# Two layers of a hybrid block on one core: residual chains split by urgency, with wide residuals and weights split ahead

## The chip, the cores and the metric

The kernel runs on one core of one Trainium2 chip. The metric is the device time of one execution in microseconds; runs are compared by their median. A core has TensorE (PE, the matmuls), VectorE (DVE), ScalarE (ACT), GpSimd (POOL), and SyncE (SP), which issues most DMAs. TensorE's clock has two levels, 1.2 and 2.4 GHz; the profile shows the granted clock as a share of the higher.

## What is computed

The input is 16 meta tokens and 512 tokens of width 1024, in float32. Two layers follow, each of the same form (cut from the reference; `s5_mixer`, `swa_attention` and `mla_mixer` are a complex linear recurrence over the tokens, attention in a window of 128, and attention with compressed keys and values):

```
for l in range(DEPTH):                                   # 2
    a = rms_norm(h, norm_pre_mix[l])
    u, q, k, v, cq, ckv, kr = split(a @ w_in[l])
    mixed = concat(rms_norm(s5_mixer(u), g_s5), rms_norm(swa_attention(q, k, v), g_swa),
                   rms_norm(mla_mixer(cq, ckv, kr), g_mla))
    h = h + rms_norm(mixed @ w_out[l], norm_post_mix[l])
    a = rms_norm(h, norm_pre_mlp[l])
    f = square(relu(a @ w_mlp_up[l])) @ w_mlp_down[l]    # 1024 -> 4096 -> 1024
    h = h + rms_norm(f, norm_post_mlp[l])
return h[:, 16:]
```

A norm multiplies by the reciprocal root of the mean square over the 1024 features of each token, and by a gain for each feature.

## The kernel before

**Layout.** All activations lie with features on the 128 partitions: `h` is 128 x 8 x tokens (feature 128k + p). The tokens go in two halves, A with 272 and B with 256, so each product has 272 or 256 columns. A norm's sum over the features is a matmul against a column of ones (`colsum`, L205) after the eight squared slices were added up: Squares on ScalarE, additions on VectorE (L200).

**Products.** A weight block is 128 outputs by 1024 inputs; each of its halves is one DMA of 128x512 floats (`raw`, issued by SP, L130). A float32 product is made of three fp32r products: ScalarE copies the half to the rounded `hi`, VectorE subtracts it to get `lo` (the split, L135, named `w`), and TensorE runs hi x hi, hi x lo, lo x hi, so 12 matmuls per half and 24 per block (L163, named `d` or `bu`). Activations are split in the same way: `gains` gives hi on ScalarE, with the gain as its scale, and lo on VectorE (L173, eight of each), `split` does it for the MLP's inner values (L170, `slot<-rl`). Some products of the first layer run in plain float32 (L155).

**Chains.** Between the products stand chains that use VectorE and ScalarE alone, but for the column sum:
- `norm_in(l, half)`: gains, sum of squares, column sum, reciprocal root `r`; `w_in` needs the gains first, and `r` when its columns are evicted (L403, L421, L447).
- `chain_mid(l, half)` after w_out: sum of squares over w_out's results (`big`), column sum, root (L215 to L217), `residual`, gains, then sum of squares and column sum of the new `h`.
- `chain_end(l, half)` after the MLP: the same up to `residual`, with a square more (L879, L881).

`residual` takes, for each of eight slices, one multiplication by `r` (L791) and one multiplication by the gain with addition to `h` (L792):

```
V.tensor_tensor(src[:, k, :n], src[:, k, :n], r[:, :n], op=ALU.mult)
V.scalar_tensor_tensor(h[hf][:, k, o:o + n], src[:, k, :n], sm(l, gn, k), h[hf][:, k, o:o + n], ...)
```

**Order.** The program is written as generators. `weave(main, sides)` takes steps of a main stream of products and, for every microsecond of its estimated cost, lets the side streams spend `rate` microseconds: the S5 recurrence (`RS`), the attentions (`RA`), the preparation of the next layer's S5 tables (`RP`). A scheduler at build time then orders each engine's instructions by the place where they were written and by priority: a part in `tc.high_priority(offset=HP)` is moved ahead by that offset; all chains have HP = 100, weight splits HW = 50. Each engine works through its list in order.

One layer runs so: norm and w_in of half A (11 blocks); w_in of half B; w_out of A; chain_mid of A; up and part of down of A's first MLP chunk; w_out of B; chain_mid of B; the chunks of the MLP (four of 8 up and 8 down blocks), first for B alone, then A and B together, then A alone. The last B blocks of a layer (`late`) run in the next layer: CU = 6 of them between the next layer's norm_in of A and its w_in, the rest behind that w_in. Half B's chain_end and norm_in of layer 1 run under w_out(1,0). In layer 1, w_in of B stands behind w_out(1,0) and chain_mid(1,0) (`WB[1] = 0`), and its first two blocks are the S5 input u, evicted by L421; S5 then takes transposes (L499, `y`), its input product (L513, `bu`), the recurrence on VectorE (L518 to L544, the scan at L534) and its output product (L557).

**Buffers named below.** `raw`, `w`: a weight half and its split. `slot`: split activations. `rl`: two buffers of 128x272 in the MLP. `ch`: three rows of a chain. `big0`, `big1`: results of w_out and of the MLP, by half. `kv`: the attention's keys and values of a layer.

The functions, with the profile's line numbers:

## Time and profile before

| | us |
|---|---|
| median of 3 runs | 1291.93 (1291.27 to 1293.69) |
| the profiled execution | 1289.2 |
| its span | 1287.4 |
| TensorE busy | 1217.5 (95%) |
| VectorE busy | 868.7 (67%) |
| ScalarE busy | 848.6 (66%) |
| chain that ended last, by engine | PE 47%, DVE 6%, ACT 2% |

A time in square brackets at the end of a timeline's row is how long the engine had stood before it, and the arrow names what ended that. Rows with "x8" hold eight instructions in a row; their time goes from the start of the first to the end of the last, and successive instructions overlap a little on one engine. TensorE's busy time counts matmuls at the lower clock in full.

### The profile page before, as it was taken

To read this page: it belongs to the slowest core of one execution; us is meant where nothing else is said; L and a number is where in the kernel's file an instruction comes from. 1 tells how busy PE (TensorE), PEld (TensorE's weight loads), DVE (VectorE), ACT (ScalarE), POOL (GpSimd) and SP (SyncE) were. 2 spreads that over 40 slices of the span, in tenths; PEclk is the share of its full clock that TensorE was granted. 3 is DMA by queue.
4 is the path that set the end of the run, shared out by engine and by line. 5 is a ranking of instruction groups with operands and counts; after the bars stand their busy time and mean duration, and the time that the engine had idled before them with its cause. 6 is when DMAs were issued, how large, how long until landed. Compare 5 with 4: busy or idle time off the path is not lost.

```text
span 1287.4 us, 27466 instructions
## 1 busy us (share of the span) xinstructions
PE 1217.5 (95%) x10256; PEld 1133.8 (88%) x10256; DVE 868.7 (67%) x2056; ACT 848.6 (66%) x1977; POOL 41.9 (3%) x103
## 2 busy tenths in 40 slices
PE   6999998999999999799999986999999999999995
PEld 4787876899999999788999985778989999999985
DVE  7888768789656656857766787766685333344775
ACT  6787777987764666766786674798675532534662
POOL 4000002000000000000000000000000000000000
PEclk9999998999999999899999996999999999999998
DMA  7223423254666656433456641314646332334652
GB/s 225 83 83 100 149 67 91 82 179 131 193 181 173 179 168 179 116 122 92 125 162 185 194 147 33 108 58 123 181 148 189 91 97 86 97 100 129 186 184 85
DMA packets 93237, 170.55 MB, mean 132 GB/s; under 512 B 10960, under 2 KB 14032, under 8 KB 93104
## 3 DMA queue, kind: packets, MB, share of 16 engines
q1 hardware_dynamic: 90288, 161.62, 42.3%
q0 software_dynamic: 2816, 7.18, 1.7%
q8 instruction: 81, 1.33, 0.4%
q14 instruction: 52, 0.43, 0.1%
HBM read 166.66 MB, written 2.10 MB: 131 GB/s over the span
## 4 chain that ended last, share of the span: by engine, by line
PE 47%; DVE 6%; ACT 2%; issue 1%; DMA 1%; DVEq 0%; ACTq 0%
PE d L163 33%; PE bu L163 7%; PE o L763 1%; DVE h L792 1%; DVE big L791 1%; PE pt L739 1%; PE s L680 1%; PE s L715 1%; DVE w L135 1%; PE bu L513 1%; DMA raw<-in_wblk 1%; ACT ch L126 1%; DVE slot L173 1%; PE o L205 1%; ACT w L126 0%
## 5 line engine op out<-in xcount | busy, mean ns | idle before, releaser
L163 PE MATMUL d<-slot,w 128*128 128x256 f32 (+1 forms) x6984 | 914.4, 289 | 22.1 <-ACT rl L126 6.2
L163 PEld LDWEIGHTS d<-slot,w 128*128 128x128 f32 x6984 | 867.5, 190 | 47.9 <-issue 11.9
L135 DVE TENSOR_TENSOR w<-raw,w 128x512 fp32r<-128x512 f32 x582 | 400.1, 690 | 214.7 <-ACT w L126 206.8
L126 ACT ACTIVATE w<-raw 128x512 fp32r<-128x512 f32 x582 | 364.1, 627 | 254.8 <-PE d L163 174.6
L170 DVE TENSOR_TENSOR slot<-rl,slot 128x256 fp32r<-128x256 f32 (+1 forms) x128 | 54.0, 427 | 62.4 <-ACT slot L126 60.6
L163 PE MATMUL bu<-slot,w 128*128 128x256 f32 x768 | 92.9, 280 | 0.0
L163 PEld LDWEIGHTS bu<-slot,w 128*128 128x128 f32 x768 | 91.4, 188 | 0.0
L126 ACT ACTIVATE rl<-d 128x256 f32<-128x256 f32 (+1 forms) x112 | 42.3, 377 | 29.8 <-PE d L163 28.6
L126 ACT ACTIVATE slot<-rl 128x256 fp32r<-128x256 f32 (+1 forms) x128 | 52.6, 418 | 2.6
L126 ACT ACTIVATE rl<-rl 128x256 f32<-128x256 f32 (+1 forms) x128 | 52.5, 417 | 1.8
L200 DVE TENSOR_TENSOR ch<-ch 128x256 f32<-128x256 f32 (+1 forms) x112 | 47.5, 424 | 5.1 <-ACT ch L126 3.9
L155 PE MATMUL d<-slot,raw 128*128 128x272 f32 x144 | 37.7, 408 | 10.8 <-DMA raw<-in_wblk 10.8
L865 DVE TENSOR_TENSOR big<-d,big 128x256 f32<-128x256 f32 (+1 forms) x80 | 34.3, 429 | 16.3 <-PE d L163 12.7
L155 PEld LDWEIGHTS d<-slot,raw 128*128 128x128 f32 x144 | 27.7, 198 | 17.6 <-ACT ch L126 10.7
L126 ACT ACTIVATE slot<-h,small 128x256 fp32r<-128x256 f32 (+2 forms) x72 | 33.2, 505 | 14.1 <-DVE h L792 9.4
L126 ACT ACTIVATE ph<-pt 128x512 f32<-128x512 f32 (+2 forms) x66 | 36.3, 550 | 7.2 <-PE pt L739 6.2
L680 PE MATMUL s<-kv,slot 128*128 128x512 f32 (+1 forms) x64 | 31.3, 571 | 2.1 <-DVE slot L447 1.7
L126 ACT ACTIVATE ch<-h 128x256 f32<-128x256 f32 (+1 forms) x64 | 25.1, 413 | 10.7 <-DVE ch L200 9.5
L126 ACT ACTIVATE big<-d 128x256 f32<-128x256 f32 (+1 forms) x64 | 23.9, 374 | 8.5 <-PE d L163 8.4
L126 ACT ACTIVATE ch<-big 128x256 f32<-128x256 f32 (+1 forms) x64 | 25.9, 412 | 5.4 <-DVE big L865 4.8
L173 DVE SCALAR_TENSOR_TENSOR slot<-h,small,slot 128x256 fp32r<-128x256 f32 (+1 forms) x64 | 27.9, 481 | 0.8 <-ACT slot L126 0.8
L792 DVE SCALAR_TENSOR_TENSOR h<-big,small,h 128x256 f32<-128x256 f32 (+1 forms) x64 | 28.4, 480 | 0.0
(641 smaller groups left out, 1101.3 us busy)
## 6 DMA issues: line engine op xcount, KB each, us to landing
raw<-in_wblk SPq DMA_DIRECT2D x600, 256.0 KB, 2.7
ph<-in_wuq POOLq DMA_DIRECT2D x8, 256.0 KB, 3.5
h<-in_xT SPq DMA_DIRECT2D x4, 272.0 KB, 4.0
h<-in_xT SPq DMA_DIRECT2D x1, 1024.0 KB, 11.3
ph<-in_wukv POOLq DMA_DIRECT2D x4, 256.0 KB, 3.6
u<-in_wglu POOLq DMA_DIRECT2D x4, 256.0 KB, 3.3
out<-h SPq DMA_DIRECT2D x1, 1024.0 KB, 5.7
out<-h SPq DMA_DIRECT2D x4, 256.0 KB, 2.2
```

The lines of the kernel that those rows point to most:

```text
L126: S.activation(out, in_, func, **kw)
L135: V.tensor_tensor(w[:, 1].rearrange("p k m -> p (k m)"), raw, f32(hi), op=ALU.subtract)
L155: PE.matmul(ps[:, :n], lhsT=raw[:, k * P:(k + 1) * P], rhs=a[:, 4 * q + k, :n], start=q + k == 0, stop=q + k == 4)
L163: PE.matmul(ps[:, :n], lhsT=w[:, wi, k, :], rhs=a[:, ai, 4 * q + k, :n], start=i == 0, stop=i == 23)
L170: V.tensor_tensor(lo, src, f32(hi), op=ALU.subtract)
L173: V.scalar_tensor_tensor(lo, src, gain, f32(hi), op0=ALU.mult, op1=ALU.subtract)
L200: V.tensor_tensor(acc, acc, sq, op=ALU.add)
L205: PE.matmul(ps[:, :n], lhsT=ones[:, 0:1].to_broadcast([P, P]), rhs=acc, start=True, stop=second is None)
L513: PE.matmul(bu[:, c, j * K:j * K + K], lhsT=s5["wt"][:, c, 4 * o + j, :], rhs=u4[:, o, j * K:j * K + K], start=True, stop=True)
L680: PE.matmul(sp[:, :2 * nk].rearrange("p (e k) -> p e k", e=2), lhsT=M["q"][:, c0:c0 + P], rhs=L["k2"][:, :, ks:ks + nk], start=True, stop= ...
L792: V.scalar_tensor_tensor(h[hf][:, k, o:o + n], src[:, k, :n], sm(l, gn, k), h[hf][:, k, o:o + n], op0=ALU.mult, op1=ALU.add)
L865: V.tensor_tensor(ac[:, b, :n], ps[:, :n], ac[:, b, :n], op=ALU.add)
```

## The change

- `residual` works on two slices at a time (GR = 2): four multiplications by `r`, read twice over as a broadcast, and four additions to `h`, none with a gain.
- The gain goes elsewhere. `w_out` evicts each block twice on ScalarE, as a Square into `rl` and as a copy with the gain as scale; VectorE adds up the Squares block by block (L832), with one buffer for the sum and one for all Squares behind the first. `chain_end` has eight scalings on ScalarE (`ac`) written behind its column sum.
- The priorities: `chain_mid` has HC = 100 up to its gains and HM = 30 behind them; `norm_in` has 100 for the gains and HS = 60 for its sum and root.
- NBC = (0, 2): in layer 1, two blocks of w_in of half B are written ahead of chain_mid(1,0).
- CU 6 to 9 and RS[0] from 1.6 to 1.2 for half A's S5 of layer 0.
- `keep`: the halves of the first two `late` blocks are loaded and split in the last eight blocks of layer 0, into the room of `kv`, which is free from there to the next layer's `open_layer`; the S5 preparation is woven into 40 blocks, not 48.

```diff
 FULL_C0 = ()
-RS = ((1.6, 0.5), (0.8, 0.8))
+RS = ((1.2,.5),(.8,.8))
 RP = 0.25
...
 ORD = ((2, 3, 4, 5, 10, 6, 7, 8, 9, 0, 1), (0, 1, 2, 3, 4, 5, 10, 6, 7, 8, 9))
-CU = 6
+CU = 9
+NBC = (0, 2)
+HC = (100,100)
+HM = 30
+GR = 2
+HS = 60
+NREST = 48
+KB = 8
 WB = (10, 0)
...
-    def load_half(l, b, q):
+    kept = {}
+
+    def keep(l, b0, nb):
+        room = mk(mem, [P, KVW], F32R, "kv")
+        for i in range(2 * nb):
+            w = room[:, 1024 * i:1024 * i + 1024].rearrange("p (x k m) -> p x k m", x=2, k=4)
+            kept[l, b0 + i // 2, i % 2] = load_half(l, b0 + i // 2, i % 2, w)
+            yield 0
+
+    def load_half(l, b, q, w=None):
+        if (l, b, q) in kept:
+            return kept.pop((l, b, q))
         raw = mk(wraw, [P, 4 * P], F32, "raw")
         nc.sync.dma_start(out=raw, in_=wblk[l * NB + b, q])
-        w = mk(wsp, [P, 2, 4, P], F32R, "w")
+        if w is None:
+            w = mk(wsp, [P, 2, 4, P], F32R, "w")
         hi = w[:, 0].rearrange("p k m -> p (k m)")
...
         with tc.high_priority(offset=HP):
-            return norm_in_(l, hf, n, tag)
-
-    def norm_in_(l, hf, n, tag):
-        a, _ = gains(l, hf, 0, n, "g_in", (l, hf) in FULL_IN)
-        tm = chain_tmp()
-        acc = sumsq(tm, lambda k: h[hf][:, k, :n], KD, n)
-        r = mk(nt, [P, 272], F32, "rc", bufs=2)
-        rsqrt(tm, colsum(acc, n, tag), n, D, r[:, :n])
+            a, _ = gains(l, hf, 0, n, "g_in", (l, hf) in FULL_IN)
+        with tc.high_priority(offset=HS):
+            tm = chain_tmp()
+            acc = sumsq(tm, lambda k: h[hf][:, k, :n], KD, n)
+            r = mk(nt, [P, 272], F32, "rc", bufs=2)
+            rsqrt(tm, colsum(acc, n, tag), n, D, r[:, :n])
         return a, r
...
-    def residual(l, hf, src, r, gn):
+    def residual(l, hf, src, r):
         o, n = span(l, hf)
-        for k in range(KD):
-            V.tensor_tensor(src[:, k, :n], src[:, k, :n], r[:, :n], op=ALU.mult)
-            V.scalar_tensor_tensor(h[hf][:, k, o:o + n], src[:, k, :n], sm(l, gn, k), h[hf][:, k, o:o + n],
-                                   op0=ALU.mult, op1=ALU.add)
+        rb = r[:, :n].unsqueeze(1).to_broadcast([P, GR, n])
+        for k in range(0, KD, GR):
+            x, y = src[:, k:k + GR, :n], h[hf][:, k:k + GR, o:o + n]
+            V.tensor_tensor(x, x, rb, op=ALU.mult)
+            V.tensor_tensor(y, y, x, op=ALU.add)
...
-    def w_out(l, hf, mixed, o, b0, b1):
+    def w_out(l, hf, mixed, o, tm):
         n = span(l, hf)[1]
-        for b in range(b0, b1):
+        for b in range(KD):
             ps, = gemm(l, NB_IN + b, [(mixed, n)])
-            act(o[:, b, :n], ps[:, :n])
+            sq = tm[min(b, 1)][:, :n]
+            act(sq, ps[:, :n], AF.Square)
+            act(o[:, b, :n], ps[:, :n], scale=sm(l, "g_pmix", b))
+            if b:
+                V.tensor_tensor(tm[0][:, :n], tm[0][:, :n], sq, op=ALU.add)
             yield cost(l, hf, FULL_OUT, n)
...
-    def chain_mid(l, hf, ob, tag):
-        with tc.high_priority(offset=HP):
-            return chain_mid_(l, hf, ob, tag)
-
-    def chain_mid_(l, hf, ob, tag):
+    def chain_mid(l, hf, ob, tm, tag, hp=HP):
         o, n = span(l, hf)
-        tm = chain_tmp()
-        acc = sumsq(tm, lambda k: ob[:, k, :n], KD, n)
-        r = rsqrt(tm, colsum(acc, n, tag), n, D)
-        residual(l, hf, ob, r, "g_pmix")
         full = (l, hf) in FULL_C0
-        a, room = gains(l, hf, o, n, "g_mlp", full)
-        tm = chain_tmp()
-        acc = sumsq(tm, lambda k: h[hf][:, k, o:o + n], KD, n)
-        rc = mk(nt, [P, 272], F32, "rc", bufs=2)
-        recip(tm, rc[:, :n], colsum(acc, n, tag), n, D)
+        with tc.high_priority(offset=hp):
+            acc = tm[0][:, :n]
+            tm = chain_tmp()
+            r = rsqrt(tm, colsum(acc, n, tag), n, D)
+            residual(l, hf, ob, r)
+            a, room = gains(l, hf, o, n, "g_mlp", full)
+        with tc.high_priority(offset=min(hp, HM)):
+            tm = chain_tmp()
+            acc = sumsq(tm, lambda k: h[hf][:, k, o:o + n], KD, n)
+            rc = mk(nt, [P, 272], F32, "rc", bufs=2)
+            recip(tm, rc[:, :n], colsum(acc, n, tag), n, D)
         return dict(a=a, rc=rc, ac=obuf(hf), n=n, full=full, room=room)
...
         ps = colsum(acc, n, tag)
+        for k in range(KD):
+            act(ac[:, k, :n], ac[:, k, :n], scale=sm(l, "g_pmlp", k))
         c2 = tm[0][:, :n]
...
         V.tensor_tensor(r, r, rc[:, :n], op=ALU.mult)
-        residual(l, hf, ac, r, "g_pmlp")
+        residual(l, hf, ac, r)
...
+    def part(g, n):
+        for _, us in zip(range(n), g):
+            yield us
+
     def take(g, n):
...
             o = obuf(0)
-            yield from staged(s5_ok, w_out(l, 0, M[0]["mixed"], o, 0, 8))
-            A.update(chain_mid(l, 0, o, "d" if WB[l] == NB_IN else "o"))
+            tm = [mk(nt, [P, 272], F32, "rl", bufs=2) for _ in range(2)]
+            yield from staged(s5_ok, w_out(l, 0, M[0]["mixed"], o, tm))
+            yield from staged(s5_ok, part(winB[0], NBC[l]))
+            A.update(chain_mid(l, 0, o, tm, "d" if WB[l] == NB_IN else "o", HC[l]))
             yield from staged(s5_ok, winB[0])
...
         o = obuf(1)
-        run(w_out(l, 1, M[1]["mixed"], o, 0, 8))
-        B = chain_mid(l, 1, o, "o")
+        tm = [mk(nt, [P, 272], F32, "rl", bufs=2) for _ in range(2)]
+        run(w_out(l, 1, M[1]["mixed"], o, tm))
+        B = chain_mid(l, 1, o, tm, "o")
         run(down(l, CA[l], [A], CD[l], 8))
...
         rest = seq(mlp(l, CA[l] + 1, CZ[l], [A, B]), mlp(l, CZ[l], NCH, [A]))
-        weave(staged(0, rest), ((layers[l + 1]["prep"], RP, 0),) if l < DEPTH - 1 else ())
+        if l < DEPTH - 1:
+            weave(staged(0, part(rest, NREST - KB)), ((layers[l + 1]["prep"], RP, 0),))
+            kp = keep(l, NB_IN + NB_OUT + 16 * CZ[l], 2)
+            for i, us in enumerate(rest):
+                if i % (KB // 4) == 0:
+                    next(kp, None)
+            run(kp)
+        else:
+            run(rest)
         chain_end(l, 0, A, "o")
```

Lines below 791 move by 7 to 19, those behind by up to 37: L135 is now L154, L163 L182, L173 L192, L170 L189, L200 L219, L205 L224, L791/792 L810/811, L421 L438, L499 L516, L513 L530.

On VectorE, at chain_mid of half A in layer 1, before (`h_85` is half A's h, `big_1500` or `big_1499` the results of w_out, `slot_9999` or `slot_9919` S5's input u):

```order
L217 TENSOR_TENSOR ch_9916<-ch_9916 128x256
L791 TENSOR_TENSOR big_1499_9627<-big_1499_9627,ch_9916 128x256 x2
L792 SCALAR_TENSOR_TENSOR h_85<-big_1499_9627,small_94,h_85 128x256 x2
L791 TENSOR_TENSOR big_1499_9627<-big_1499_9627,ch_9916 128x256 x2
L792 SCALAR_TENSOR_TENSOR h_85<-big_1499_9627,small_94,h_85 128x256 x2
L791 TENSOR_TENSOR big_1499_9627<-big_1499_9627,ch_9916 128x256 x2
L792 SCALAR_TENSOR_TENSOR h_85<-big_1499_9627,small_94,h_85 128x256 x2
L791 TENSOR_TENSOR big_1499_9627<-big_1499_9627,ch_9916 128x256 x2
L792 SCALAR_TENSOR_TENSOR h_85<-big_1499_9627,small_94,h_85 128x256 x2
L173 SCALAR_TENSOR_TENSOR slot_9956<-h_85,small_94,slot_9956 128x256 x8
L200 TENSOR_TENSOR ch_9973<-ch_9973 128x256
L421 TENSOR_TENSOR slot_9999<-d_10002,rc_9618 128x64x4
```

and now:

```order
L154 TENSOR_TENSOR w_10117<-raw_10115,w_10117 128x512
L438 TENSOR_TENSOR slot_9919<-d_9922,rc_9603 128x64x4
L234 SCALAR_TENSOR_TENSOR ch_10055<-o_10056,ch_10055 128x256
L154 TENSOR_TENSOR w_10134<-raw_10132,w_10134 128x512
L235 TENSOR_SCALAR ch_10055<-ch_10055 128x256
L236 TENSOR_TENSOR ch_10055<-ch_10055 128x256
L154 TENSOR_TENSOR w_10238<-raw_10236,w_10238 128x512
L810 TENSOR_TENSOR big_1500_9612<-big_1500_9612,ch_10055 128x2x256 x2
L811 TENSOR_TENSOR h_85<-h_85,big_1500_9612 128x2x256 x2
L810 TENSOR_TENSOR big_1500_9612<-big_1500_9612,ch_10055 128x2x256 x2
L811 TENSOR_TENSOR h_85<-h_85,big_1500_9612 128x2x256 x2
L192 SCALAR_TENSOR_TENSOR slot_10072<-h_85,small_94,slot_10072 128x256 x8
```

The residual is four rows of two wide operations, and the first eviction of u (L438) stands ahead of it; the second one is next behind the eight L192.

On TensorE, at the same place, from the end of w_out, before (`o` is the column sum of the chain, `y` and `bu` are S5's transposes and input product):

```order
L163 MATMUL d_10002<-slot_9585,w_10005 128x256 x12
L163 MATMUL d_10002<-slot_9585,w_10022 128x256 x12
L163 MATMUL d_10038<-slot_9585,w_10041 128x256 x12
L163 MATMUL d_10038<-slot_9585,w_10058 128x256 x3
L205 MATMUL o_9932<-ch_9916,ones 128x256
L163 MATMUL d_10038<-slot_9585,w_10058 128x256 x9
L499 MATMUL y_10075<-slot_9999,ident 32x64 x16
L163 MATMUL d_10135<-slot_9585,w_10138 128x256 x3
```

and now:

```order
L182 MATMUL d_9922<-slot_9570,w_9925 128x256 x12
L182 MATMUL d_9922<-slot_9570,w_9942 128x256 x3
L224 MATMUL o_10056<-rl_9613,ones 128x256
L182 MATMUL d_9922<-slot_9570,w_9942 128x256 x9
L182 MATMUL d_9958<-slot_9570,w_9961 128x256 x12
L182 MATMUL d_9958<-slot_9570,w_9978 128x256 x12
L516 MATMUL y_9995<-slot_9919,ident 32x64 x16
L182 MATMUL d_10114<-slot_9570,w_10117 128x256 x4
L530 MATMUL bu_10031<-u_1555_9994,wt_5516 128x64 x8
```

Before, 39 matmuls stand between w_out and the column sum, now 15; S5's first input product stands between the matmuls of a third block of w_in, and the second transposes 20 matmuls further on.

On VectorE, at chain_end of half A in layer 0 with the norm of layer 1 (`rl_6638` or `rl_6633` is an inner value of the MLP's late block), before:

```order
L791 TENSOR_TENSOR big_409_2519<-big_409_2519,ch_6511 128x272
L173 SCALAR_TENSOR_TENSOR slot_6554<-h_85,small_94,slot_6554 128x272 x2
L792 SCALAR_TENSOR_TENSOR h_85<-big_409_2519,small_92,h_85 128x272
L791 TENSOR_TENSOR big_409_2519<-big_409_2519,ch_6511 128x272 x2
L173 SCALAR_TENSOR_TENSOR slot_6554<-h_85,small_94,slot_6554 128x272
L792 SCALAR_TENSOR_TENSOR h_85<-big_409_2519,small_92,h_85 128x272 x2
L200 TENSOR_TENSOR ch_6571<-ch_6571 128x272
L170 TENSOR_TENSOR slot_6602<-rl_6638,slot_6602 128x256
```

and now:

```order
L192 SCALAR_TENSOR_TENSOR slot_6559<-h_85,small_94,slot_6559 128x272 x2
L810 TENSOR_TENSOR big_411_2513<-big_411_2513,ch_6516 128x544
L192 SCALAR_TENSOR_TENSOR slot_6559<-h_85,small_94,slot_6559 128x272 x2
L811 TENSOR_TENSOR h_85<-h_85,big_411_2513 128x544
L810 TENSOR_TENSOR big_411_2513<-big_411_2513,ch_6516 128x544
L189 TENSOR_TENSOR slot_6607<-rl_6633,slot_6607 128x256
L811 TENSOR_TENSOR h_85<-h_85,big_411_2513 128x544
L192 SCALAR_TENSOR_TENSOR slot_6559<-h_85,small_94,slot_6559 128x272 x2
```

The correction row (L170, now L189) stood behind all of the residual; now it is ahead of the last wide addition and of four gains.

On VectorE at w_out(1,0), with chain_end(0,1) and norm_in(1,1) beside it (`h_86` is half B's h), there now stands:

```order
L810 TENSOR_TENSOR big_613_3687<-big_613_3687,ch_9527 128x2x256
L192 SCALAR_TENSOR_TENSOR slot_9570<-h_86,small_94,slot_9570 128x256 x4
L811 TENSOR_TENSOR h_86<-h_86,big_613_3687 128x512
L810 TENSOR_TENSOR big_613_3687<-big_613_3687,ch_9527 128x2x256
L832 TENSOR_TENSOR rl_9613<-rl_9613,rl_9614 128x256
L192 SCALAR_TENSOR_TENSOR slot_9570<-h_86,small_94,slot_9570 128x256 x2
```

and on ScalarE there:

```order
L133 ACTIVATE rl_9614<-d_9652 128x256
L133 ACTIVATE big_1500_9612<-d_9652,small_94 128x256
L133 ACTIVATE w_9769<-raw_9767 128x512
L133 ACTIVATE w_9786<-raw_9784 128x512
L133 ACTIVATE slot_9570<-h_86,small_94 128x256 x4
L133 ACTIVATE w_9807<-raw_9805 128x512
L133 ACTIVATE w_9824<-raw_9822 128x512
L133 ACTIVATE slot_9570<-h_86,small_94 128x256 x2
L133 ACTIVATE ch_9587<-h_86 128x256 x3
L133 ACTIVATE rl_9614<-d_9690 128x256
L133 ACTIVATE big_1500_9612<-d_9690,small_94 128x256
```

The add L832 frees `rl_9614` for the next Square of w_out, `rl_9614<-d_9690`, which stands on ScalarE behind weight splits, six gains and three Squares of the norm.

## Rows read from the trace of the kernel before

**Rows 1.** The page, busy time by engine, and tenths of 40 slices of 32 us.

```profile
PE 1217.5 (95%) x10256; PEld 1133.8 (88%) x10256; DVE 868.7 (67%) x2056; ACT 848.6 (66%) x1977; POOL 41.9 (3%) x103
...
DVE  7888768789656656857766787766685333344775
```

**Rows 2.** Table by stretch: window, length, busy us and count, clock, DMA, GB/s.

```profile
320.00:500.00 180.00, 179.94 (x1453) 179.03 (x1452) 112.03 (x190) 111.68 (x231) 1.33 (x3) 1.00 0.61 179
500.00:560.00 60.00, 52.57 (x367) 48.59 (x366) 44.88 (x97) 42.58 (x97) 1.64 (x3) 0.94 0.46 134
...
765.00:805.00 40.00, 27.12 (x302) 24.21 (x300) 31.13 (x78) 20.25 (x50) 0.00 (x0) 0.74 0.22 64
```

**Rows 3.** Waits of TensorE: waiting and releaser, us in all, times, longest.

```profile
PE y L499 <- DVE slot L421: 12.1, 1, 12.1
...
PE d L163 <- DVE w L135: 5.3, 5, 2.6
PE d L163 <- DVE slot L173: 4.3, 2, 2.3
```

**Rows 4.** Timeline 765 to 803: start, us, engine, operation, [idle before, releaser].

```profile
770.37 0.70 PE L205 MATMUL o<-ch,ones 128*128 128x256 f32 x2 [0.34 <-DVE ch L200]
...
774.24 0.76 DVE L791 TENSOR_TENSOR big<-big,ch 128x256 f32<-128x256 f32 x2
774.91 0.87 DVE L792 SCALAR_TENSOR_TENSOR h<-big,small,h 128x256 f32<-128x256 f32 x2
...
780.09 3.25 DVE L173 SCALAR_TENSOR_TENSOR slot<-h,small,slot 128x256 fp32r<-128x256 f32 x8
...
784.25 1.08 PE L499 MATMUL y<-slot,ident 128*32 128x64 f32 x32 [12.12 <-DVE slot L421]
784.36 0.62 DVE L421 TENSOR_TENSOR slot<-d,rc 128x256 f32<-128x256 f32 x1
...
792.64 0.69 DVE L518 TENSOR_TENSOR wP<-bu,tab 128x512 f32<-128x512 f32 x1 [5.28 <-PE bu L513]
...
800.92 0.42 DVE L544 SCALAR_TENSOR_TENSOR wP<-wQ,wP 128x252 f32<-128x252 f32 x1
```

**Rows 5.** Timeline 1232 to 1249, VectorE and TensorE after the residual.

```profile
1233.55 0.68 DVE L135 TENSOR_TENSOR w<-raw,w 128x512 fp32r<-128x512 f32 x1
...
1234.29 0.73 PE L163 MATMUL d<-slot,w 128*128 128x256 f32 x4 [1.89 <-DVE w L135]
...
1234.49 1.28 DVE L135 TENSOR_TENSOR w<-raw,w 128x512 fp32r<-128x512 f32 x2
```

**Rows 6.** Timeline 508 to 531, residual, correction row L170 and TensorE.

```profile
515.36 0.78 DVE L791 TENSOR_TENSOR big<-big,ch 128x272 f32<-128x272 f32 x2
...
524.31 0.41 DVE L170 TENSOR_TENSOR slot<-rl,slot 128x256 fp32r<-128x256 f32 x1
...
525.36 5.28 PE L163 MATMUL d<-slot,w 128*128 128x256 f32 x27 [6.18 <-ACT rl L126]
```

**Rows 7.** Timeline 194.5 to 211, residual, TensorE and gains.

```profile
200.89 0.79 DVE L791 TENSOR_TENSOR big<-big,ch 128x272 f32<-128x272 f32 x2
...
202.70 1.27 PE L163 MATMUL d<-slot,w 128*128 128x272 f32 x4 [2.26 <-ACT slot L126]
...
207.01 3.38 DVE L173 SCALAR_TENSOR_TENSOR slot<-h,small,slot 128x272 fp32r<-128x272 f32 x8
...
207.55 3.77 PE L163 MATMUL d<-slot,w 128*128 128x272 f32 x15 [2.05 <-DVE slot L173]
```

**Rows 8.** The page, costliest groups: ScalarE's Squares of a chain.

```profile
L126 ACT ACTIVATE ch<-big 128x256 f32<-128x256 f32 (+1 forms) x64 | 25.9, 412 | 5.4 <-DVE big L865 4.8
```

**Rows 9.** Timeline 1271 to the end, the last column sum.

```profile
1273.21 0.70 PE L205 MATMUL o<-ch,ones 128*128 128x256 f32 x2 [1.49 <-DVE ch L200]
```

**Rows 10.** Timeline 737 to 760, TensorE.

```profile
749.98 1.20 PE L163 MATMUL d<-slot,w 128*128 128x256 f32 x8 [1.03 <-ACT big L126]
753.76 6.26 PE L163 MATMUL d<-slot,w 128*128 128x256 f32 x38 [2.57 <-DVE w L135]
```

## Prediction

> **What bounds it now.** I read the busy line and the tenths first. TensorE is busy 1217.5 of 1287.4 us, so the kernel is bound by matmuls except where TensorE stands; VectorE runs at six to nine tenths in the first ten slices of 32 us [rows 1]. Then the table by stretches: 320 to 500 is full, 179.94 of 180 us busy at the full clock. Its 1453 matmuls give 179.94 / 1453 = 0.124 us each, so 24 of them (one weight block, 128x256) take 2.97 us. In 765 to 805 TensorE is busy only 27.12 of 40 us, and the granted clock is 0.74; with two levels, 1.2 and 2.4 GHz, that means 2 x 0.26 x 40 = 20.8 us at the lower one. In 500 to 560 it is 52.57 of 60 us at 0.94, so 7.2 us at the lower level [rows 2]. The list of TensorE's waits names what ends them: one of 12.1 us for VectorE's L421, one of 6.2 us for an eviction on ScalarE, 5.3 us in five for weight splits, 4.3 us in two for L173 [rows 3, 6]. All of them stand beside a residual chain. So the sum is made by chains, and what a chain is shortened by counts only where TensorE waits for it.
>
> **Layer 1, middle chain of half A (the largest term).** Call E the end of w_out. Before, 24+15 matmuls stand between it and the column sum at 770.37; 39 x 0.124 = 4.8, and 0.34 us idle, so E is about 765.2. From the sum to the residual are 774.24 - 770.37 = 3.87 us, the residual takes 780.09 - 774.24 = 5.85, the eight gains 3.25, and only then come both L421 that free TensorE; S5 is through with its first group at 800.92 + 0.42 = 801.34 [rows 4]. That is E + 36.1. After, the order of VectorE has the first of the two evictions (now L438) ahead of the residual, and the order of TensorE has the S5 input product of the first group beside other blocks; the column sum stands behind 15 matmuls, not 39. The terms: Square and add of the last block and the sum itself about 2.2 (15 x 0.124 = 1.9 of matmuls beside it); 3.9 to the residual as before; the wide residual 4.8 (below); gains 3.25; second eviction 0.6; and what before stood between that eviction and the end of the group, 801.34 - 784.36 = 17.0, less the 5.28 us in which VectorE waited for the input product [rows 4], so 11.7. Sum 26.5, against 36.1: 9.6 us less, and about 10 with a part of the half-clock time. TensorE's wait does not vanish. Its cover, two blocks and the first group, ends about E + 11, and the second eviction is done at E + 14.8, so a wait of some 4 us is next, named by L438. Bounds: -4, if S5 behind the chain loses what the early start gave (the whole 5.28 is waited again); -12, if the wait of 12.12 goes and all else stays.
>
> **Wide residuals.** A chain had 8 pairs of 128x256; two L791 start 774.91 - 774.24 = 0.67 apart from the next operation, so 0.335 each, and a pair 5.85 / 8 = 0.73, so L792 0.40. Now there are 8 operations of 128x512. The trace has none of this kind in f32 with a broadcast operand; nearest is the weight split of the same size: alone 0.68, two in a row 1.28, so 0.60 apart [rows 5]. 8 x 0.60 = 4.8, and 1.05 saved. Bounds: 0 (a wide operation costs two narrow ones, 8 x 0.67 = 5.4, and a broadcast read costs the rest) and 1.5. The order issues two L810 before the first L811, so the first piece of h is ready after 1.8 us, not 0.67 + 0.47 = 1.14, and the first gain comes 0.7 us later; the last comes earlier, and TensorE needs all eight.
>
> The Trainium skill would give less: its page Perfetto Trace Analysis, section Optimizing Scalar/DVE Operations, puts about 60 ns on each VectorE instruction for access to SBUF, so by it 8 instructions fewer are an estimated 0.48 us. The same section says that where an engine isn't full but causes bubbles, breaking instructions up can finish work sooner, which speaks against this edit. By the first the sum below would lose about 4 us over seven chains; the rows give 0.13 us an instruction, and I go by them.
>
> **The end of layer 0 (chain_end and next norm).** TensorE waits 6.18 us until 525.36. The eviction that ends it goes behind L170 at 524.31, which is 8.95 us after the residual's start at 515.36 [rows 6]. In that time VectorE does 16 residual operations, gains and one addition. After, the order puts it (L189) behind seven wide ones, 7 x 0.60 x 272/256 = 4.45, and four gains, 4 x 3.25/8 = 1.6: 6.1 us, so 2.8 sooner. On ScalarE the eviction still stands behind gains and Squares, so I count 1.7 of these on TensorE. The two weight blocks split ahead take four splits out of the chain, which is why nothing but the chain stands there. Of the 7.2 us at the lower level, 3.6 us are lost; half back is 1.8. Sum -3.5, from -1 (the eviction stays behind the last gains) to -6. The three further blocks of CU, 3 x 2.97 = 8.9 us, cover the norm behind it; TensorE's idle time in 500 to 560 is 7.4 and the wait 6.2, so at most 1.2 is there to win, within the bounds.
>
> **The middle chain of layer 0, half A.** Residual 207.01 - 200.89 = 6.1 (not counting its gains) against 8 x 0.64 = 5.1: 1.0. The waits there are 2.26 and 2.05 [rows 7]. The Square now reads PSUM, so one copy of about 0.4 [rows 8] goes ahead of the column sum. With about 1 us of half clock: -2.5, from -4 to +2 (the later first gain of 0.7 counts twice where TensorE takes the pieces as they come).
>
> **Three chains more.** Middle of layer 1 half B 1.05 + 0.4; end of layer 1 half A 1.05 (its 1.89 us wait for a split behind the residual [rows 5]); the tail 1.05, with nothing beside it, from the column sum at 1273.21 to the end [rows 9]. Sum -3.5, from -5 to -1.
>
> **Costed at nothing.** The end of layer 0, half B, runs under w_out of layer 1 and waits 1.03 and 2.57 [rows 10]. There the chain is shorter, but each w_out block now has its Square in one buffer until VectorE's add L832; the first add stands behind residual and four gains, and ScalarE, in order, holds behind the next Square. I expect the two to balance: 0, from -1 to +4. The scalings that take the gain out of the residual: 32 in the down loops, 32 x 0.41 = 13 us [rows 8] on ScalarE, which idles a third of the span; the last is behind the column sum, where ScalarE waits; if uncovered, 0.4 a chain. The other 32 take the place of the copies of w_out, one for one. RS 1.6 to 1.2: S5 of layer 0 is fed a quarter slower and ends about two blocks later, 6 us; VectorE is mostly full there, whichever order is taken. 0, within half of that, -3 to +3.
>
> **Sum.** -10 - 3.5 - 2.5 - 3.5 = -19.5. The profiled execution is 1289.2 (span 1287.4 and 1.8 around it): 1269.7. The median of the runs lies 2.7 above it, 1291.9: 1272.4, say 1272.
>
> **Rivals.**
> - The middle chain of layer 1 gives only its lower bound: the second eviction, still behind residual and gains, gates everything that follows, and S5's wait for its product comes back. For it: 4.8 + 3.25 us stay ahead of L438. Against: the first group needs none of this. -4 in place of -10: 1278. Chance 0.2.
> - Slower, by one mechanism: the single Square buffer of w_out. Every Square waits for the add of the block before, and ScalarE's weight splits queue behind it, so TensorE waits for weights. It decides in the w_outs of half A, where VectorE has S5 (layer 0) or a chain (layer 1) ahead of the adds: 16 blocks. From 19.5 / 16 = 1.2 us a block all is eaten; at 1.4 the time is 1292 + 3 = 1295. For it: one add may stand behind up to 4.8 + 3.25 = 8 us; VectorE's tenths there. Against: a block takes 2.97 us of TensorE, and the order lets only one add stand behind a chain. Chance 0.08.
> - The gains are there but swallowed: VectorE, full in the first third, and the S5 work that slides with RS give back 6, the half clock stays, the middle chain gives 4 only, the w_out of layer 1 costs 4, which leaves -19.5 + 6 + 3 + 6 + 4, about 0: 1292. Chance 0.05.
> - The small size by the skill's figure for an instruction, 4 us less of gain: 1276. Chance 0.05.
>
> **How the numbers follow.** Forecast 0.62, own range 1264 to 1280. Faster is 0.62 + 0.2 + 0.05 = 0.87, same 0.05, slower 0.08; 0.2%, 2.6 us, is what a measurement can tell here from none. The bounds of the terms sum to 31 below and little above before; the range takes in the second case and most bounds: 1261 to 1286.
>
> **What would show it.** Right: in the list of TensorE's waits the 12.1 for the eviction falls to about 4, the clock of the stretch behind w_out of layer 1 rises above 0.85, L810 and L811 in a row start 0.60 apart, the wait of 6.2 falls to under 5, the tail is 1 us shorter. Wrong: TensorE waits for ScalarE's copies or for weights inside w_out with ScalarE waiting for L832; L810 of 0.75 or more; the wait of 12 in two parts with the same sum.

## The result and the profile after

The changed kernel takes 1275.89 us (1275.31 to 1277.09, four runs) against 1291.6 beside it on the same chip: a ratio of 0.9878, 95% interval 0.9861 to 0.9895, or 15.7 us less. The forecast was 1272; the measured time lies inside its range, 1261 to 1286. The profiled execution has a span of 1273.5 us against 1287.4, 13.9 less, and a mean clock of 0.986 against 0.977.

Both executions can be cut at the same column sums: of half A's chain end of layer 0, half B's chain end of layer 0, half B's middle chain of layer 1, half A's last chain end, and the last of all. The tables by stretch have the columns of [rows 2]; the counts of matmuls show that the stages hold the same work. The kernel before:

```profile
0.00:508.94 508.94, 485.92 (x4013) 440.43 (x4013) 379.64 (x985) 364.86 (x858) 34.26 (x81) 0.99 0.48 141
508.94:737.80 228.86, 220.51 (x1945) 205.74 (x1945) 162.57 (x370) 162.83 (x385) 5.10 (x14) 0.99 0.48 142
737.80:935.66 197.86, 180.02 (x1547) 159.92 (x1548) 140.07 (x342) 144.96 (x351) 2.56 (x8) 0.94 0.37 112
935.66:1221.71 286.05, 283.27 (x2380) 281.60 (x2380) 142.84 (x266) 145.00 (x319) 0.00 (x0) 0.99 0.42 124
1221.71:1273.21 51.50, 47.05 (x371) 45.79 (x372) 35.65 (x72) 29.19 (x64) 0.00 (x0) 0.97 0.50 152
1273.21:1287.40 14.19, 0.70 (x2) 0.29 (x2) 7.93 (x21) 1.75 (x4) 0.00 (x0) 0.63 0.22 74
```

The changed kernel:

```profile
0.00:508.44 508.44, 485.63 (x4012) 440.82 (x4013) 379.93 (x973) 373.40 (x872) 32.05 (x76) 0.99 0.47 143
508.44:735.35 226.91, 220.80 (x1946) 205.65 (x1946) 159.60 (x358) 164.19 (x390) 8.67 (x19) 0.99 0.46 141
735.35:922.15 186.80, 176.45 (x1547) 157.49 (x1547) 136.38 (x326) 144.25 (x351) 2.55 (x8) 0.97 0.38 117
922.15:1209.24 287.09, 285.15 (x2380) 283.44 (x2380) 141.87 (x258) 148.48 (x327) 0.00 (x0) 0.99 0.41 123
1209.24:1260.16 50.92, 45.52 (x371) 44.26 (x371) 34.41 (x64) 32.84 (x72) 0.00 (x0) 1.00 0.50 155
1260.16:1273.50 13.34, 0.70 (x2) 0.30 (x2) 6.90 (x13) 1.78 (x5) 0.00 (x0) 0.64 0.24 79
```

The differences of the lengths are -0.50, -1.95, -11.06, +1.04, -0.58 and -0.85 us, together -13.9. One stage made four fifths of it, the one with the middle chain of half A in layer 1. A length less TensorE's busy time is what it stood: in that stage 17.8 before and 10.4 after; the other 3.6 us are busy time, at a mean clock of 0.97 in place of 0.94. In the fourth it stood less, 2.8 and 1.9, and was yet slower: its busy time rose from 283.27 to 285.15 for the same 2380 matmuls, which is the clock.

TensorE's waits in the changed kernel, in the form of [rows 3]:

```profile
PE d L182 <- ACT slot L133: 5.6, 4, 3.8
PE d L182 <- ACT rl L133: 4.7, 2, 4.2
PE d L182 <- ACT big L133: 4.5, 2, 3.9
PE y L516 <- DVE slot L438: 3.2, 1, 3.2
```

The 12.1 us for L421 are 3.2 for L438, the 6.2 for the eviction `rl` is 4.2 in the longest, the 5.3 for splits on VectorE are 1.1. Others have grown: those for evictions of w_out (`big`) from 1.5 to 4.5, those for gains on ScalarE (`slot`) from 2.8 to 5.6, those for ScalarE's part of a split from 0.5 to 2.1.

At the middle chain of half A in layer 1, the rows that answer to [rows 4]:

```profile
765.90 0.70 PE L224 MATMUL o<-rl,ones 128*128 128x256 f32 x2
...
767.69 0.64 DVE L438 TENSOR_TENSOR slot<-d,rc 128x256 f32<-128x256 f32 x1 [0.76 <-PE d L182]
...
770.43 1.29 DVE L810 TENSOR_TENSOR big<-big,ch 128x512 f32<-128x512 f32 x2
...
771.64 1.29 DVE L811 TENSOR_TENSOR h<-h,big 128x512 f32<-128x512 f32 x2
...
775.25 3.25 DVE L192 SCALAR_TENSOR_TENSOR slot<-h,small,slot 128x256 fp32r<-128x256 f32 x8
...
778.42 0.59 DVE L438 TENSOR_TENSOR slot<-d,rc 128x256 f32<-128x256 f32 x1
...
787.82 0.42 DVE L561 SCALAR_TENSOR_TENSOR wP<-wQ,wP 128x252 f32<-128x252 f32 x1
```

The first L438 stands ahead of the residual, the second behind the gains. The residual takes 775.25 - 770.43 = 4.82 us, and two wide operations 771.64 - 770.43 = 1.21 from start to start, 0.605 each. From the column sum to the end of S5's first group (787.82 + 0.42 = 788.24) are 788.24 - 765.90 = 22.3 us; before they were 801.34 - 770.37 = 31.0.

At the end of layer 0, against [rows 6]:

```profile
513.68 1.36 DVE L810 TENSOR_TENSOR big<-big,ch 128x544 f32<-128x544 f32 x2
...
519.84 0.42 DVE L189 TENSOR_TENSOR slot<-rl,slot 128x256 fp32r<-128x256 f32 x1
...
522.50 0.36 ACT L133 ACTIVATE rl<-d 128x256 f32<-128x256 f32 x1
...
522.91 4.77 PE L182 MATMUL d<-slot,w 128*128 128x256 f32 x24 [4.23 <-ACT rl L133]
```

L189 starts 519.84 - 513.68 = 6.16 us behind the residual's start, where L170 started 8.95 behind it. The eviction that TensorE waits for starts 522.50 - 513.68 = 8.82 behind it, where it was 9.59 (524.95 - 515.36): it now stands 2.2 us behind the end of L189, after gains and Squares on ScalarE.

In the middle chain of layer 0, against [rows 7]:

```profile
196.52 1.64 DVE L235 TENSOR_SCALAR ch<-ch 128x272 f32<-128x272 f32 x1
...
197.03 0.97 POOL L348 MEMSET tt<- 128x1024 f32 x1
...
201.96 1.83 PE L182 MATMUL d<-slot,w 128*128 128x272 f32 x4 [3.82 <-ACT slot L133]
...
204.99 5.00 PE L182 MATMUL d<-slot,w 128*128 128x272 f32 x20 [1.20 <-DVE slot L192]
```

The chain step L235, a `tensor_scalar` of 128x272, takes 1.64 us while GpSimd's memset runs. TensorE's two waits are 3.82 and 1.20, where they were 2.26 and 2.05: the chain ends earlier, but TensorE also comes to it earlier, with two matmuls fewer done.

### The profile page after: what moved, and what is told of

The parts are those of the page before. It is cut to its first block, busy times and chain, and to the rows that moved or that the text cites. A ratio compares the mean times of both kernels' runs of the same rounds, so it can differ in the third digit from the quotient of the medians.

```text
span 1273.5 us, 27373 instructions
## 1 busy us (share of the span) xinstructions
PE 1214.2 (95%) x10256; PEld 1131.9 (89%) x10256; DVE 859.1 (67%) x1992; ACT 864.9 (68%) x2012; POOL 43.3 (3%) x103
## 4 chain that ended last, share of the span: by engine, by line
PE 45%; DVE 4%; ACT 3%; DMA 1%; issue 1%; DVEq 0%; ACTq 0%
PE d L182 32%; PE bu L182 7%; PE o L780 1%; DMA raw<-in_wblk 1%; PE pt L756 1%; PE s L697 1%; DVE big L810 1%; ACT w L133 1%; ACT slot L133 1%; DVE w L154 1%; DVE h L811 1%; PE s L732 1%; ACT ch L133 1%; PE o L224 0%; ACT rl L133 0%
## 5 line engine op out<-in xcount | busy, mean ns | idle before, releaser
L182 PE MATMUL d<-slot,w 128*128 128x256 f32 (+1 forms) x6936 | 911.8, 289 | 20.6 <-ACT slot L133 5.6
L182 PEld LDWEIGHTS d<-slot,w 128*128 128x128 f32 x6936 | 861.7, 190 | 48.9 <-issue 13.9
L154 DVE TENSOR_TENSOR w<-raw,w 128x512 fp32r<-128x512 f32 x578 | 396.9, 691 | 214.3 <-ACT w L133 204.7
L133 ACT ACTIVATE w<-raw 128x512 fp32r<-128x512 f32 x578 | 360.3, 627 | 233.8 <-PE d L182 168.4
L189 DVE TENSOR_TENSOR slot<-rl,slot 128x256 fp32r<-128x256 f32 (+1 forms) x128 | 54.2, 428 | 60.4 <-ACT slot L133 58.2
L182 PE MATMUL bu<-slot,w 128*128 128x256 f32 x768 | 92.9, 280 | 0.0
L182 PEld LDWEIGHTS bu<-slot,w 128*128 128x128 f32 x768 | 91.4, 188 | 0.0
L133 ACT ACTIVATE rl<-d 128x256 f32<-128x256 f32 (+1 forms) x144 | 54.2, 376 | 33.6 <-PE d L182 31.9
L219 DVE TENSOR_TENSOR ch<-ch 128x256 f32<-128x256 f32 (+1 forms) x84 | 35.8, 426 | 5.9 <-ACT ch L133 5.9
L192 DVE SCALAR_TENSOR_TENSOR slot<-h,small,slot 128x256 fp32r<-128x256 f32 (+1 forms) x64 | 27.7, 484 | 1.0 <-ACT slot L133 1.0
L732 PE MATMUL s<-kv,slot 96*128 96x264 f32 (+3 forms) x80 | 26.3, 410 | 0.5 <-DVE nm L611 0.4
L780 PE MATMUL o<-ph,vs 128*64 128x128 f32 x256 | 22.7, 286 | 0.0
L810 DVE TENSOR_TENSOR big<-big,ch 128x512 f32<-128x512 f32 (+1 forms) x32 | 21.0, 693 | 0.1
```

The lines of the kernel that those rows point to most:

```text
L133: S.activation(out, in_, func, **kw)
L154: V.tensor_tensor(w[:, 1].rearrange("p k m -> p (k m)"), raw, f32(hi), op=ALU.subtract)
L182: PE.matmul(ps[:, :n], lhsT=w[:, wi, k, :], rhs=a[:, ai, 4 * q + k, :n], start=i == 0, stop=i == 23)
L189: V.tensor_tensor(lo, src, f32(hi), op=ALU.subtract)
L192: V.scalar_tensor_tensor(lo, src, gain, f32(hi), op0=ALU.mult, op1=ALU.subtract)
L219: V.tensor_tensor(acc, acc, sq, op=ALU.add)
```

## Experiments

The theory for the runs: the middle chain of layer 1 gained by the two blocks ahead of it, the other places by shorter chains, and what a shorter chain gives is only what TensorE's next wait leaves. The rivals stand in each expectation. All ratios are to the kernel before, run beside each kernel; the changed kernel's is 0.9878 (0.9861 to 0.9895), and 0.001 is 1.3 us.

**Without the two blocks.**

```diff
-NBC = (0, 2)
+NBC = (0, 0)
```

> The changed kernel with NBC = (0, 0): w_in of half B no longer goes ahead of the middle chain of layer 1. Theory: the two blocks written ahead carry about half of the gain at that place; both evictions L438 stand again behind residual and gains, about 15 us after the end of w_out, TensorE has only 48 matmuls (6 us) to do till then, so a wait of 8 to 9 us in place of 3.2 and a longer stretch at the lower clock: 5 to 8 us slower than the changed kernel, 1281 to 1284. Rival: the gain there comes from the early column sum and the wide residual, NBC is worth 1 us: 1277.

Measured: 0.9906 (0.9889 to 0.9923), some 3.6 us slower than the changed kernel, with intervals that just overlap. The mechanism is plain in the list of waits:

```profile
PE y L516 <- DVE slot L438: 8.3, 1, 8.3
```

8.3 us for L438, as expected, in place of 3.2. By the profile the whole is 4.2 us slower (span 1277.7), and the stage of this chain 3.4 (190.16 for 186.80). Both theories are off in size: the two blocks are worth about 4 here, not 5 to 8 and not 1.

**The two blocks alone, in the kernel before.**

```diff
+NBC = (0, 2)
...
+            yield from staged(s5_ok, part(winB[0], NBC[l]))
             A.update(chain_mid(l, 0, o, "d" if WB[l] == NB_IN else "o"))
```

> The kernel before with NBC = (0, 2) alone, nothing else changed. Its order has both evictions L421 ahead of the residual, as the column sum still comes late. Theory: the wait of 12.1 for L421 goes to under 2 us and most of the 20 us at the lower clock with it: 7 to 10 us faster than before, about 1283. Rival: the chain is what counts, and its late column sum stays, so at most 4 us: 1288.

Measured: 0.9945 (0.993 to 0.996), 7.1 us faster than before: the theory's lower end. In the profile the stage of this chain is 8.4 us shorter (189.47 for 197.86). The wait for L421 is gone; the longest at that place is now S5's second input product, which waits for the recurrence behind the residual (a timeline's row):

```profile
791.49 1.72 PE L514 MATMUL bu<-u,wt 128*128 128x64 f32 x7 [4.37 <-DVE wQ L520]
```

So the blocks alone give 7 us where nothing else is changed, and 4 where the early column sum and the wide residual have already taken the wait of 12.1 to 8.3. The two do not add up.

**Second eviction ahead of the residual.**

```diff
-HC = (100,100)
+HC = (100,70)
```

> The changed kernel with HC = (100, 70): on VectorE, the second eviction of u (L438) now stands ahead of the residual of the middle chain of layer 1; nothing else of that chain is moved. Theory: the 3.2 us that TensorE waits for L438 are gone, and the chain is 0.6 us later, covered by the S5 products: 2 to 3 us faster than the changed kernel, 1273. Rival: the wait only moves behind the chain (the S5 recurrence waits for VectorE, which is in the residual): 0, 1276.

Measured: 0.9871 (0.9853 to 0.9889), the same as the changed kernel. The rival holds; the wait for L438 has become one for L536, the recurrence behind the residual:

```profile
784.39 1.94 PE L530 MATMUL bu<-u,wt 128*128 128x64 f32 x8 [2.77 <-DVE wQ L536]
```

**The adds of w_out first.**

```diff
+                with tc.high_priority(offset=400):
+                    V.tensor_tensor(tm[0][:, :n], tm[0][:, :n], sq, op=ALU.add)
```

> The changed kernel with the adds of w_out's Squares (L832) at a higher priority: at w_out(1,0) they stand ahead of and between the wide residual operations of the chain end of half B, not behind them. Theory: TensorE's wait of 3.9 us for ScalarE's eviction there falls under 2 us, as the next Square no longer waits for an add behind the residual: 1 to 3 us faster than the changed kernel, 1273.5. Rival: the residual is later by three adds of 0.4 us and the gains that w_in needs with it, which gives it back: 0, 1276.

Measured: 0.9873 (0.9855 to 0.9891), the same. The wait of 3.9 us for an eviction in w_out(1,0) (3.87 in the timeline) is there two waits, of 0.87 and 2.30; before the change it was two as well, of 1.03 and 2.57 [rows 10]. The first row is the Square of the third block:

```profile
744.53 0.37 ACT L133 ACTIVATE rl<-d 128x256 f32<-128x256 f32 x1
...
752.11 2.29 PE L182 MATMUL d<-slot,w 128*128 128x256 f32 x9 [2.30 <-DVE w L154]
```

This Square starts 744.53 - 736.56 = 8.0 us behind the column sum of half B's chain end, where in the changed kernel it was 748.65 - 735.35 = 13.3, on ScalarE behind six gains and three Squares of the norm. There the add had ended 0.8 us before it, at 747.82, so at its start the Square waited for its place in ScalarE's list and not for the add. To have it earlier gives nothing: a wait for a split takes the place of that for the eviction.

**Narrow and wider residuals.**

```diff
-GR = 2
+GR = 1
```

> The changed kernel with GR = 1: the residual is 16 additions and multiplications of 128x256, without gains, not 8 of twice the width. Theory: 16 x 0.335 = 5.4 us a chain against 4.8, 0.55 us more at each of the five chains that TensorE or the end waits for: 2 to 3 us slower than the changed kernel; in the tail, where nothing is beside it, 0.5. Rival: the first piece of h is ready sooner and ScalarE's gains start earlier, as a page on breaking instructions up says, so no more than 0.5 slower, or faster.

Measured: 0.9928 (0.991 to 0.9946), 6.4 us slower than the changed kernel, more than twice what the theory expects. By the profile it is 9.7 us slower, 4.0 of them in TensorE's busy time, at a mean clock of 0.981 in place of 0.986. The two longest waits at chain ends beside other work grew by more than a chain's 0.55 us, from 4.2 to 5.9 and from 3.9 to 5.7:

```profile
PE d L182 <- ACT rl L133: 5.9, 1, 5.9
PE d L182 <- ACT big L133: 5.7, 1, 5.7
```

```diff
-GR = 2
+GR = 4
```

> The changed kernel with GR = 4: the residual is four operations of 128x1024. Its order at the end of layer 0 has L189 behind all eight gains and two additions, not behind four gains and ahead of the last addition. Theory: width saves another 0.25 us or less for each halving, and what the pieces let slip in between decides: TensorE's waits of 4.2 and 3.9 us at the two chain ends beside other work grow by 1 to 2 us each, so 1 to 4 us slower than the changed kernel. Rival: fewer instructions decide, as between GR = 1 and 2: 1 to 2 faster.

Measured: 0.9919 (0.9902 to 0.9936), 5.3 us slower, more than the 1 to 4 expected; the waits of 4.2 and 3.9 are 5.3 each, as the theory had it. The end of layer 0 in the timeline:

```profile
514.80 2.50 DVE L810 TENSOR_TENSOR big<-big,ch 128x1088 f32<-128x1088 f32 x2
...
524.22 0.42 DVE L189 TENSOR_TENSOR slot<-rl,slot 128x256 fp32r<-128x256 f32 x1
...
524.68 0.38 ACT L133 ACTIVATE rl<-d 128x256 f32<-128x256 f32 x1
```

Two operations of 128x1088 take 2.50 us; four of 128x544, 0.64 apart in the changed kernel, take some 2.6, so width saves little beyond GR = 2. L189 stands behind all gains, 524.22 - 514.80 = 9.4 us after the residual's start. With GR = 1 it is as late, 527.15 - 517.16 = 10.0 us, behind all the gains and three additions that found room between the small pieces:

```profile
517.16 0.79 DVE L810 TENSOR_TENSOR big<-big,ch 128x272 f32<-128x272 f32 x2
...
527.15 0.43 DVE L189 TENSOR_TENSOR slot<-rl,slot 128x256 fp32r<-128x256 f32 x1
...
527.67 0.36 ACT L133 ACTIVATE rl<-d 128x256 f32<-128x256 f32 x1
```

TensorE's wait here follows the eviction `rl<-d`. Behind the residual's start it begins at 8.82 us with GR = 2, at 527.67 - 517.16 = 10.51 with GR = 1 and at 524.68 - 514.80 = 9.88 with GR = 4; the waits are 4.23, 5.90 and 5.32. With GR = 1 and 4 it begins less than 0.1 us behind the end of L189, which reads this buffer. So of the 1.7 us that GR = 1 loses at this place some 0.55 are longer operations and the rest is the place of L189 in VectorE's list. How much of the whole 6.4 and 5.3 us comes by places in the lists is not shown: larger pieces also let ScalarE's gains start later (in the middle chain of layer 0 TensorE waits 5.5 us for them with GR = 4, not 3.8), and part is the clock.

**RS, CU and the blocks split ahead, each undone.**

```diff
-RS = ((1.2,.5),(.8,.8))
+RS = ((1.6, 0.5), (0.8, 0.8))
```

> The changed kernel with RS[0] as before, 1.6 for S5 of half A in layer 0. Theory: what the middle chain of layer 0 gained (its second column sum was 3.7 us earlier) was gone at 320 us, where only 0.3 were left, because the S5 work that RS = 1.2 put off came due; with 1.6 TensorE is at the same place of its work 1 to 2 us earlier at 320 us, and the whole 1 to 2 faster. Rival: RS moves nothing that bounds, 0 within 1.

Measured: 0.9889 (0.9867 to 0.9911). The theory falls: RS did not eat the gain of layer 0; with 1.6 the run is no faster, though the first wait there is 2.4 us in place of 3.8.

```diff
-CU = 9
+CU = 6
```

> The changed kernel with CU = 6: three late blocks fewer between the norm of half A of layer 1 and its w_in. Theory: they covered the norm's column sum and root, at most 1.2 us: 0 to 1.2 slower. Rival: the three blocks give w_in's S5 and attention work of layer 1 more to lie beside when they stand behind it, so CU = 6 is as fast or up to 1 faster.

Measured: 0.9874 (0.9852 to 0.9895): no difference.

```diff
-            weave(staged(0, part(rest, NREST - KB)), ((layers[l + 1]["prep"], RP, 0),))
-            kp = keep(l, NB_IN + NB_OUT + 16 * CZ[l], 2)
...
+            weave(staged(0, rest), ((layers[l + 1]["prep"], RP, 0),))
```

> The changed kernel without the two blocks split ahead into the key area, and with the preparation woven into all 48 blocks as before. Theory: four splits of 0.6 us on VectorE and as many on ScalarE stand again in the chain at the end of layer 0; TensorE's wait of 4.2 us there becomes 5.5 to 6.5: 1.5 to 2.5 slower. Rival: the chain waits for ScalarE's steps there anyway and the splits lie in these gaps: 0.5 or less.

Measured: 0.9891 (0.987 to 0.9912), 1.7 us slower, which the intervals do not separate from none; the wait at that place does, 5.5 us where it was 4.2. The residual starts 514.85 - 508.42 = 6.43 us behind its column sum there, as before the change (515.36 - 508.94 = 6.42), and 513.68 - 508.44 = 5.24 behind it in the changed kernel: the four splits stand in between.

**The last chain end.** In the changed kernel SP issues the store of half A's result behind the residual, and the loads behind that store (timeline, SP and TensorE):

```profile
1220.16 0.61 SPq L1028 DMA_DIRECT2D out<-h  x1
...
1220.80 0.74 PE L182 MATMUL d<-slot,w 128*128 128x256 f32 x4 [0.87 <-DVE w L154]
...
1227.18 4.03 PE L182 MATMUL d<-slot,w 128*128 128x256 f32 x32 [1.88 <-ACT w L133]
```

The wait for the split has gone from 1.89 [rows 5] to 0.87, and 1.88 for a split whose load came late is next.

```diff
-        if l == DEPTH - 1:
-            nc.sync.dma_start(out=outT[:, :, 0:256], in_=h[0][:, :, NM:])
         late = behind(l, CZ[l], FL[l], B)
+        if l == DEPTH - 1:
+            for k in range(0, KD, 2):
+                take(late, 3)
+                nc.sync.dma_start(out=outT[:, k:k + 2, 0:256], in_=h[0][:, k:k + 2, NM:])
```

> The changed kernel with the store of half A's result (1 MB, one DMA that SP issues behind the residual of the last chain end of half A) cut in four and issued three weight blocks apart, each behind the loads of those blocks. Theory: the loads that queued behind that store on SP are issued at once, the 1.9 us wait for a split that waits for a load and the two of 0.5 us behind it go: 2 to 3 us faster than the changed kernel, 1273.5. Rival: the loads wait for their buffers, which the standing TensorE holds, so the wait stays: 0.

Measured: 0.9842 (0.9822 to 0.9862), 4.7 us faster than the changed kernel. The second wait is gone:

```profile
1220.08 12.79 PE L182 MATMUL d<-slot,w 128*128 128x256 f32 x104 [0.20 <-DVE w L154]
```

Between the same two column sums as in the fifth stage above, which took 50.92 us, are now 48.28, so 2.6 us are won at this place:

```profile
1207.60:1255.88 48.28, 45.24 (x371) 44.18 (x371) 34.23 (x64) 32.61 (x72) 0.00 (x0) 1.00 0.54 162
```

Of the 4.5 us by the profile the rest is mostly at the middle chain of half B, in the clock (last section).

**GpSimd's memset first.**

```diff
+        nc.gpsimd.memset(tt, 0.0)
         nc.gpsimd.dma_start(out=braw, in_=bD[l])
         nc.gpsimd.dma_start(out=vt[:, CL - 1], in_=cD[l])
-        nc.gpsimd.memset(tt, 0.0)
```

> The changed kernel with GpSimd's memset of tt (128x1024, 0.97 us) issued ahead of its two DMA issues, not behind them. In the changed kernel's trace the chain step L235 of the middle chain of layer 0 takes 1.64 us, not 0.29, while that memset runs. Theory: a two-times faster form of VectorE's instruction waits for GpSimd's memset; with the memset 1.1 us earlier it ends before L235, which takes 0.29 again, the chain is 1.3 us shorter, and the whole 0.5 to 1.3 faster. Rival: another instruction of VectorE meets the memset instead (L583 or the like), and the time is the same.

Measured: 0.9847 (0.9827 to 0.9867), 4 us faster by the runs, while the profiled execution, at 1274.4, is not faster than that of the changed kernel. L235 still meets the memset's end, for 0.58 us, and TensorE's wait falls from 3.82 to 2.77:

```profile
196.11 0.58 DVE L235 TENSOR_SCALAR ch<-ch 128x272 f32<-128x272 f32 x1
...
200.49 1.63 PE L182 MATMUL d<-slot,w 128*128 128x272 f32 x4 [2.77 <-ACT slot L133]
```

The one us at the place is shown; where the rest of the runs' 4 us comes from is open. In the profile TensorE stands 2.0 us less in the first stage (20.8 for 22.8), but is busy 2.7 longer there: from 300 to 320 the granted clock is 0.91, where the changed kernel has 1.00.

**Both.**

> The changed kernel with both: the store of half A's result in four pieces behind later loads, and GpSimd's memset ahead of its DMA issues. Theory: the two places are 1000 us apart and add up, 2.6 us at the last chain end and 0.8 at the middle chain of layer 0: 3 to 4 us faster than the changed kernel and 1 us faster than the late store alone, about 0.983 of before. Rival: the 0.8 us of layer 0 shift the later stretches at the lower clock and are not seen in the whole: as the late store alone, 0.984.

Measured: 0.9818 (0.9797 to 0.9839), the lowest ratio, 23 us below the kernel before beside it (1295.7). Its own median, 1272.85, is not below the 1271.92 of the late store alone, its profiled span, 1271.5, is above that one's 1269.0, and the intervals overlap, so whether the two add up is not settled.

## Why the prediction was right, and where not

- **Middle chain of layer 1, -10.** The stage gave -11.1, with the wait of 4 us named by L438 (3.2). The cause is mixed as stated: the two blocks alone give 7, without them 4 are lost. No run undoes the early column sum or the lower priorities by themselves, so how they share the rest with the wide residual is read from the trace and not shown. The chain was better than the sum had it: the end of w_out is at 765.90 - 1.9 = 764.0, and S5's first group is through 24.2 us behind it, for 26.5. The step that was off is the last: from the second eviction's start to the group's end the sum has 0.6 + 11.7, and 788.24 - 778.42 = 9.8 were measured. It counted the eviction twice, as 784.36 is its start, and kept the five additions of 2.54 us (L200, from 784.81) that stood between it and S5's first row; now that row, L535, starts 0.76 us behind the eviction's start and the additions stand between S5's own. Of the gain 3.6 us are the clock (0.96 from 765 to 805, for 0.74), where the sum had 0.4.
- **Wide residual, 1.05 a chain.** 4.82 us in place of 5.85: right to a tenth, and 0.60 apart, as the split of the same size. But as the worth of the edit it was mis-sized: 6.4 us lie between GR = 1 and 2. The step that fell short took an operation's time for its worth; at the end of layer 0 what the pieces let in between, in VectorE's list, counted for more.
- **End of layer 0, -3.5.** L189 was 2.8 us sooner as worked out (6.16 for 6.1) and the wait 1.95 shorter (1.7 forecast), but that the two fit is luck. Only 0.77 of the 2.8 reached the eviction (8.82 for 9.59); the other 1.18 are the four splits taken out of the chain ahead of the residual (5.24 for 6.42), which the sum gave no size, and without which the wait is 5.5. The time at the lower clock did halve (0.97 for 0.94 from 500 to 560), but the 1.8 us for it did not come: the busy time of the stage is 220.80 against 220.51. Before, the clock had already fallen while TensorE stood (0.76 in the 6.18 us of the wait), where it costs nothing; in the 10 us behind the wait it was 0.80 and is 0.83.
- **Middle chain of layer 0, -2.5.** -0.50 for the whole first stage. The chain was shortened, in spite of the 1.35 us that the memset took of it, and TensorE's second wait there ends 2.6 us sooner (204.99 for 207.55), with six matmuls fewer done. But TensorE came to its first wait at 201.96 - 3.82 = 198.14, not at 202.70 - 2.26 = 200.44: two products of the attention (L680, 1.13 us, behind a wait of 1.00) that it did till then before, it does later. This term counted the chain, not TensorE's work beside it.
- **Three chains more, -3.5.** -0.4 (+1.04, -0.58, -0.85). Middle of half B: the wait fell from 2.26 (one of the two that [rows 3] has for L173) to 1.28, the forecast 1 us, but an eviction added 0.59 and the clock took more (next section). Last chain end: a wait for a load took the place of that for a split, so TensorE stood 5.4 us in that stage for 4.45 before, and the 0.58 are less than the 1.53 that its busy time fell at the higher clock (1.00 for 0.97). The tail: 4.9 us of residual for 5.9; 0.85 of it reached the end.
- **Costed at nothing.** Right for the end of half B (3.87 against 1.03 + 2.57), RS and CU, and for the scalings as far as the trace shows: the last ends at 1260.19, ahead of the last residual at 1264.95, and none is in the list of TensorE's waits. The rival by w_out's single Square buffer stayed one stall of its lower kind and did not spread to 16 blocks.

By the runs the sum missed by 3.8 us of 19.5, by the profile by 5.6: the largest term gave 1.1 more than forecast and the others 6.7 less. These took a chain's length for TensorE's, and time at the lower clock for time lost. That 1275.9 is also the figure of the last rival, 1276, is chance: the price of an operation, its mechanism, was as the rows had it and not as the rival.

## What to carry to other kernels

Count a shorter chain only up to the next wait at its place, and look for that wait in what the engines have to do until then. Where an instruction stands in a list can be worth more than how long it takes: choose the width of a chain's pieces by what the scheduler puts between them, and try both neighbours. A large store behind a chain's end can stand behind the next loads in its queue; here that won 2.6 us at the place.
